# Hybrid layer with a top-4-of-32 expert FFN on one core: first norm without GpSimd, expert 0's rows in two banks, mixer matmuls reordered, another order of the tail

## The chip, the core and the metric

One core of a Trainium2 chip. The number is the device time of one execution, in microseconds (us). TensorE runs matmuls (its weight loads are counted apart), VectorE, ScalarE and GpSimd work on rows of 128 partitions, SyncE issues most DMAs. Kernels are compared by the median of several executions.

## The reference, cut to what matters

One layer in float32 on x of 512 tokens x 1024. Three mixers side by side share one input projection; their outputs are concatenated and projected, then a scaled residual and a LayerNorm; then 4 of 32 experts per token, and a second residual and LayerNorm.

```python
p = h @ w_in
mix = concat([pool_mixer(p), rwkv7_mixer(p), mlstm_mixer(p)]) @ w_out
h = layer_norm(ALPHA * h + mix, ln1_g, ln1_b)
logits = h @ router_w + router_b
top_val, top_idx = lax.top_k(logits, 4); gate = softmax(top_val)
# per expert e, over its tokens:
gu = xb @ w_gu[e] + b_gu[e]
act = glu * sigmoid(1.702 * glu) * (lin + 1)       # both halves clamped at 7
y[tokens] += gate * (act @ w_dn[e] + b_dn[e])
h = layer_norm(ALPHA * h + y, ln2_g, ln2_b)
```

## The kernel before, in words

Tokens are four tiles of 128 rows (NT = 4), features eight chunks of 128 (NK = 8). A scheduling layer orders each engine's instructions; engines then run their own list strictly in order, and wait on each other by semaphores. So the code says what depends on what, and the printed order of an engine says what stands behind a wait.

**Mixers** (up to about 347 us). The projection runs as three products of split halves (L222 to L224 for the transposed outputs, L249 to L251 for the others, in `ml_vo`). `rwkv_prep(j)` makes the operands of head pair j: two small products on a low-rank input (L559, L572), elementwise work on VectorE, a product that sums k*r for the "bonus" (L596), then `flip` transposes of v, b, k and a (L604, L613) and the state products (L618). `rwkv_scores(j)` makes per tile and head three or four 128x128 products over 64 partitions (L652); the two heads of a pair lie in partitions 0 to 63 and 64 to 127. A base loop of 31 VectorE steps (L693, L695) then inverts small blocks, a DMA and copies (L699 to L727) put its result in place, and matmuls go on with it (L756 and on). `ml_scores` does the like for the mLSTM heads.

**Output projection and first norm** (347 to 398 us). `out_proj(i, y, LATE)` adds the last part of the projection to the residual row tile `res[i]` on VectorE (L912). `ln_stats` takes mean and variance there (L1000, L1001) and an inverse root with ScalarE's Sqrt (L444 to L450); `ln_apply`, from `norm_rows`, scales on ScalarE (L1010), multiplies by the gain on VectorE (L1011) and adds the bias on GpSimd (L1012). The router works beside it (L1023 to L1056: logits, top 4, an expert mask `mkb` per tile at L1055). `route_rank` turns masks into the ranks of tokens, and those into the one-hot matrix `P0` (L1062 to L1067).

**Experts.** A ring of 18 buffers of 1 MiB holds the streamed weights: per expert eight chunks of w_gate_up and four of w_down, loaded by SyncE; a chunk's buffer is refilled when its matmuls are done. Expert e's tokens sit in 96 rows. For expert 0, `first_xT` gathers them by matmul of `res` with `P0` (L1231): tiles 0 and 1 into two banks, tile 2 into two more, tile 3 into two more, and VectorE adds the later ones (L1238). The others are gathered by indirect DMA. `gu` opens the accumulation with the bias through a one-hot `sel` (L1213, L1214, used at L1245, L1246); `gu_low` handles rows 0 to 63 (L1268), `gu_high` rows 64 to 95 (L1273), the latter after every fourth chunk. `dn` multiplies by w_down (L1309, L1314), and the scaled rows are scattered and added to `yd` in memory by GpSimd's DMA (L1319).

**Tail.** The last expert's rows never go to memory: `tail` multiplies them by one-hot matrices (L1524, L1527), per tile and half a group of two 128x512 and four 128x256 products in one bank. `tail_rows` has GpSimd's DMA queue add `yd` into `res` (L1507), with the loads of the second norm's gain and bias between. `overflow`, ahead of `tail`, holds code for experts with more than 96 tokens, behind a branch on the largest count (L1409); it does not run with these inputs, but each engine evaluates the branch. Then come residual sums (L1531), squares on ScalarE (L1537), scales, and an apply (L1557 to L1561) that is different for tiles 0, 1 and tiles 2, 3.

Of the kernel before, what the change touches and what calls it, by code (L numbers as in the profile page):

```python
# [126 lines left out]
class Trunk:  # L127
# [100 lines left out]
    def ml_vo(self):  # L228
# [9 lines left out]
        for q in (2, 0, 1):  # L238
# [4 lines left out]
            ps = [self.bank("pi" if i < 2 else "pm") for i in range(NT)]  # L243
# [114 lines left out]
    def ml_scores(self, i):  # L358
# [8 lines left out]
        for h in range(6):  # L367
            self.exp_ins = nc.scalar.activation(DW[:, h], DW[:, h], AF.Exp, bias=self.Q[:, i, 0, h:h + 1])
        for g in range(2):
            p = self.bank("pi")  # L370
            r = slice(64 * g, 64 * g + 64)
            for j in range(3):
                nc.tensor.matmul(p[:, j * 128:j * 128 + 128], self.k2[j][r, t], self.q2[j][r, t], start=True, stop=True)
            d = DW[:, g:6:2]
            nc.vector.scalar_tensor_tensor(d, p[:, :384].rearrange("p (j t) -> p j t", j=3), 1.0 / 32, d, OP.mult, OP.mult)
# [170 lines left out]
    def rwkv_prep(self, j):  # L546
# [12 lines left out]
        nc.tensor.matmul(p, self.w2t[0:64, j * 128:(j + 1) * 128], self.wdad[0:64], start=True, stop=True)  # L559
# [11 lines left out]
        pa = self.bank()  # L571
        nc.tensor.matmul(pa, self.w2t[64:128, j * 128:(j + 1) * 128], self.wdad[64:128], start=True, stop=True)  # L572
# [46 lines left out]
        for hh in range(2):  # L619
            rr = slice(64 * hh, 64 * hh + 64)  # L620
            for i in range(NT - 1):
                nc.vector.tensor_copy(self.H[i][rr, j], p[rr, 128 * i:128 * i + 128][:, rr])
        self.pj[j] = (at, bt, kt, cj)

    def rwkv_scores(self, j, first=False):
# [16 lines left out]
        for i in range(NT):  # L642
            ti = slice(i * 128, i * 128 + 128)
            tm = self.sp.tile([128, 2, 2, 128], F32, name="mkv", tag="mkv", bufs=2)
            (mab, mrb), yrk = self.M[i], self.Yrk[i]
            for hh in range(2):
                hd = 2 * j + hh
                rows = slice(64 * hh, 64 * hh + 64)
                p = self.bank()
                for q in range(1 if first else 0, 4):  # L650
                    lh, rh = prods[q]
                    nc.tensor.matmul(p[:, 128 * q:128 * q + 128], lh[rows, ti], rh[rows, ti], start=True, stop=True)  # L652
                pq = p.rearrange("p (q t) -> p q t", q=4)
# [236 lines left out]
    def out_proj(self, i, y, ks):  # L890
# [12 lines left out]
        r = self.res[i]  # L903
        for z in range(2):
# [4 lines left out]
            if ks is EARLY:  # L909
                nc.vector.scalar_tensor_tensor(r[:, c], r[:, c], ALPHA, p, OP.mult, OP.add)  # L910
            else:
                nc.vector.tensor_tensor(r[:, c], r[:, c], p, OP.add)  # L912
        if ks is LATE:
            self.mv[i] = self.ln_stats(self.sp, r)

    def norm_rows(self, i):
        self.ln_apply(self.res[i], self.mv[i], self.lng, self.lnb)
        self.nc.scalar.dma_start(self.hd[i * 128:i * 128 + 128], self.res[i])
# [210 lines left out]
    def routing_setup(self):  # L1129
# [5 lines left out]
        self.mkb = self.cp.tile([128, NT, NE], BF, name="mkb")  # L1135
        self.ro = self.cp.tile([128, 3, NT, 4], F32, name="ro")
# [53 lines left out]

    def expert_gather(self, e):
        x = self.xg[e % 2]
        self.nc.gpsimd.indirect_dma_start(out=x[0:CAP], out_offset=None, in_=self.hd,  # L1193
                                          in_offset=bass.IndirectOffsetOnAxis(ap=self.gidx[:, e:e + 1], axis=0),
                                          bounds_check=T - 1, oob_is_err=False)
# [15 lines left out]
    def expert_sel(self, e):  # L1211
        sel = self.mw.tile([128, 2, 128], F32R, name="sel", bufs=2)
# [5 lines left out]
    def first_xT(self):  # L1218
        nc = self.nc
        sel = self.expert_sel(0)  # L1220
        xT = self.mw.tile([128, NK, CAP], F32, name="xT", bufs=2)
        for tiles in ((0, 1), (2,), (3,)):
# [457 lines left out]
```

## Time and profile before

| | before |
|---|---|
| median of 3 runs | 1492.03 us (1488.74 to 1493.71) |
| profiled execution, its own time | 1492.41 us |
| its span (first to last instruction) | 1490.7 us |
| mean granted TensorE clock | 0.962 |
| TensorE busy | 1345.4 us, 90% of the span |
| VectorE, ScalarE, GpSimd busy | 466.6, 290.7, 228.2 us |
| moved by DMA | 461.67 MB |

How to read it: a busy share is a mean over stages with different limits, so the rows further down are taken by stage. "idle before" of a row is the time its engine stood still just ahead of it, with the instruction that ended it. The granted clock is a share of 2.4 GHz: 0.50 is 1.2 GHz. Matmul rows overlap: their durations do not add up to time, their distances do.

### The profile page before, as it was taken

The numbers are of one execution on the slowest core, as the hardware profiler recorded it, in microseconds if no ns is written. First come the engines' busy times: TensorE is split into PE (matmuls) and PEld (weight loads), VectorE is DVE, ScalarE is ACT, GpSimd is POOL, SyncE is SP. The second block draws the span as 40 slices with busy tenths as digits, with TensorE's granted clock in tenths as the row PEclk, the third lists the DMA queues.
The fourth block names the chain that finished last, engine by engine and source line by source line (L and its number), as shares of the span: only waits on it lengthen the run. The fifth ranks groups of instructions, "written<-read, shape, count | busy, mean of one in ns | idle before, by whom it ended". The sixth has DMA issues, their size and how long they took to land. (4 is left out here: it accounts for less than half of the span.)

```text
span 1490.7 us, 19988 instructions
## 1 busy us (share of the span) xinstructions
PE 1345.4 (90%) x7852; PEld 639.2 (43%) x7853; DVE 466.6 (31%) x1108; ACT 290.7 (20%) x611; POOL 228.2 (15%) x206
## 2 busy tenths in 40 slices
PE   7899989998899999988799999999879888899993
PEld 5677888876533433232233333333323222333322
DVE  4867497697831212111111111111111110211115
ACT  4444243353211111111001111111100110111103
POOL 1111137142301010001001111011100100010111
PEclk9999888799899999999999999999999999999996
DMA  7222123355689999999999999999999999999964
GB/s 250 70 57 71 36 68 89 118 159 205 256 341 396 393 383 404 402 398 390 395 399 398 394 398 399 402 395 391 392 387 398 395 401 394 404 396 412 401 223 127
DMA packets 95232, 461.67 MB, mean 310 GB/s; under 512 B 18137, under 2 KB 26745, under 8 KB 45962
## 3 DMA queue, kind: packets, MB, share of 16 engines
q1 hardware_dynamic: 79674, 434.57, 74.1%
q0 software_dynamic: 10880, 21.32, 6.6%
q10 hardware_dynamic: 4560, 4.15, 0.9%
q8 instruction: 82, 1.34, 0.4%
q14 instruction: 36, 0.29, 0.1%
HBM read 445.97 MB, written 18.10 MB: 311 GB/s over the span
## 5 line engine op out<-in xcount | busy, mean ns | idle before, releaser
L1268 PE MATMUL gu<-wc,xT 128*64 128x512 f32 x2048 | 486.6, 606 | 67.0 <-DMA wc<-w_gate_up 64.4
L1268 PEld LDWEIGHTS gu<-wc,xT 128*64 128x64 f32 x2048 | 143.0, 138 | 392.9 <-issue 239.5
L1281 DVE TENSOR_SCALAR glu<-gu 128x256 f32<-128x256 f32 (+1 forms) x64 | 35.6, 556 | 843.8 <-PE gu L1273 391.5
L1314 PE MATMUL dn<-wc,aT 128*64 128x512 f32 x1024 | 247.6, 603 | 4.2 <-PEq L1261 2.4
L1282 ACT ACTIVATE glu<-glu 128x256 f32<-128x256 f32 (+1 forms) x64 | 33.6, 525 | 549.6 <-DVE glu L1281 549.4
L1193 POOL DMA_INDIRECT xg<-hd,gidx x31 | 31.3, 1009 | 665.0 <-PE tr L1207 659.7
L1314 PEld LDWEIGHTS dn<-wc,aT 128*64 128x64 f32 x1024 | 65.8, 136 | 117.6 <-issue 101.3
L1319 POOL DMA_INDIRECT yd<-eo,sidx x45 | 70.1, 1557 | 276.1 <-ACT eo L1318 276.1
L1273 PE MATMUL gu<-wc,xT 128*32 128x512 f32 x960 | 111.3, 596 | 0.0
L222 PE MATMUL pi<-xhi,whi 128*128 128x512 f32 x152 | 63.7, 419 | 8.9 <-ACT whi L172 8.9
L1208 ACT ACTIVATE xT<-tr 128x384 f32<-128x384 f32 x62 | 29.9, 490 | 177.2 <-PE tr L1207 177.2
L223 PE MATMUL pi<-xlo,whi 128*128 128x512 f32 x152 | 62.8, 413 | 0.6 <-DVE xlo L173 0.6
L1273 PEld LDWEIGHTS gu<-wc,xT 128*32 128x32 f32 x960 | 27.7, 109 | 79.3 <-issue 79.3
L224 PE MATMUL pi<-xhi,wlo 128*128 128x512 f32 x152 | 61.7, 406 | 0.0
L173 POOL TENSOR_TENSOR wlo<-wraw,whi 128x512 fp32r<-128x512 f32 (+1 forms) x28 | 39.3, 1407 | 134.9 <-ACT whi L172 129.4
L1318 ACT ACTIVATE eo<-dn,gate 128x512 f32<-128x512 f32 (+1 forms) x45 | 28.0, 621 | 162.9 <-PE dn L1314 84.4
L1309 PE MATMUL dn<-wc,aT 128*32 128x256 f32 x960 | 56.1, 381 | 1.0 <-ACT aT L1296 1.0
L172 ACT ACTIVATE whi<-wraw 128x512 fp32r<-128x512 f32 (+1 forms) x54 | 33.9, 631 | 56.4 <-DMA wraw<-w_in 25.3
L1309 PEld LDWEIGHTS dn<-wc,aT 128*32 128x32 f32 x960 | 29.5, 110 | 33.3 <-issue 13.8
L1284 DVE SCALAR_TENSOR_TENSOR glu<-glu 128x256 f32<-128x256 f32 (+1 forms) x64 | 35.6, 556 | 8.4 <-ACT glu L1282 7.1
L1295 PEld LDWEIGHTS tr<-ident,glu 128*128 128x128 f32 x192 | 25.7, 208 | 28.0 <-DVE sel L1214 19.5
L222 PEld LDWEIGHTS pi<-xhi,whi 128*128 128x128 f32 x152 | 29.5, 194 | 18.2 <-ACT whi L172 8.6
(489 smaller groups left out, 1585.8 us busy)
## 6 DMA issues: line engine op xcount, KB each, us to landing
wc<-w_gate_up SPq DMA_DIRECT2D x256, 1024.0 KB
wc<-w_down SPq DMA_DIRECT2D x128, 1024.0 KB
wraw<-w_in SPq DMA_DIRECT2D x46, 256.0 KB
wraw<-w_out SPq DMA_DIRECT2D x16, 256.0 KB
xraw<-xT SPq DMA_DIRECT2D x4, 512.0 KB
res<-x SPq DMA_DIRECT2D x4, 512.0 KB
hd<-res ACTq DMA_DIRECT2D x4, 512.0 KB
res<-yd POOLq DMA_DIRECT2D x4, 512.0 KB
```

The source lines that it names most:

```text
L172: self.hi_ins = nc.scalar.activation(hi, src, AF.Copy)
L173: return (eng or nc.vector).tensor_tensor(lo, src, hi, OP.subtract)
L222: nc.tensor.matmul(p, hi, xh, start=(k == 0), stop=False)
L223: nc.tensor.matmul(p, hi, xl, start=False, stop=False)
L224: nc.tensor.matmul(p, lo, xh, start=False, stop=(k == NK - 1))
L1268: mm(p[q][64 * h:64 * h + 64], xT[:, k, 0:64], w[:, 1024 * q + 512 * h:1024 * q + 512 * h + 512], start=False, stop=(k == NK - 1))
L1273: self.nc.tensor.matmul(p[2][32 * c:32 * c + 32], xT[:, k, 64:96], w4[:, c], start=False, stop=(k == NK - 1), skip_group_check=True)
L1281: nc.vector.tensor_scalar(out[:, c], g, 7.0, None, OP.min)
L1284: nc.vector.scalar_tensor_tensor(out[:, c], ln[:, c], 1.0, out[:, c], OP.add, OP.mult)
L1309: mm(p2[32 * c:32 * c + 32], aT[:, 4 + k % 2, 32 * (k // 2):32 * (k // 2) + 32], wd[k][:, 256 * c:256 * c + 256], start=(k == 0), stop=(k ...
L1314: mm(p0[64 * h:64 * h + 64], aT[:, k % 4, 64 * (k // 4):64 * (k // 4) + 64], wd[k][:, 512 * h:512 * h + 512], start=(k == 0), stop=(k == N ...
L1319: return nc.gpsimd.indirect_dma_start(out=self.yd.rearrange("t (c f) -> (t c) f", f=w), out_offset=bass.IndirectOffsetOnAxis(ap=self.sidx[ ...
```

## The change

It does nine things. In `ml_vo` the first of three column groups takes its banks from another set. In `ml_scores` and `rwkv_scores` the products of two heads alternate, into two banks. In `rwkv_prep` both products on the low-rank input stand together, and the bonus product stands last. In the first norm, the residual add also sums the row, ScalarE makes squares of the centred row with a sum, and VectorE applies gain, scale and bias in two operations per half. `sel` of expert 0 is made during the setup of the router. `first_xT` sums all four tiles in two banks, and ScalarE copies them out. Expert 0's high rows are multiplied after each chunk. Gathers for e < 3 have no bounds check, and the fills of `xg` are gone. In the tail, the branch block moves behind it (and would redo residual and norm); the gain and bias are loaded by SyncE; for tiles 2 and 3 an identity matmul adds `res` in the bank, and ScalarE empties it with a sum; scale roots are taken for two tiles at once; all applying is VectorE's.

```diff
@@ ml_vo
-            ps = [self.bank("pi" if i < 2 else "pm") for i in range(NT)]
+            ps = [self.bank("ps" if q == 0 else "pi" if i < 2 else "pm") for i in range(NT)]
@@ rwkv_prep
         p = self.bank()
-        nc.tensor.matmul(p, self.w2t[0:64, ...], self.wdad[0:64], start=True, stop=True)
+        pa = self.bank()
+        for o, rows in ((p, slice(0, 64)), (pa, slice(64, 128))):
+            nc.tensor.matmul(o, self.w2t[rows, j * 128:(j + 1) * 128], self.wdad[rows], start=True, stop=True)
...
-        p = self.bank()
-        nc.tensor.matmul(p[32 * j:32 * j + 2], c["bd2"], r, start=True, stop=True)
-        nc.scalar.activation(self.bonT[32 * j:32 * j + 2], p[32 * j:32 * j + 2], AF.Copy)
...
+        p = self.bank()
+        nc.tensor.matmul(p[32 * j:32 * j + 2], c["bd2"], r, start=True, stop=True)
+        nc.scalar.activation(self.bonT[32 * j:32 * j + 2], p[32 * j:32 * j + 2], AF.Copy)
@@ rwkv_scores
+            ps = [self.bank() for _ in range(2)]
+            for q in range(1 if first else 0, 4):
+                lh, rh = prods[q]
+                for hh in range(2):
+                    rows = slice(64 * hh, 64 * hh + 64)
+                    nc.tensor.matmul(ps[hh][:, 128 * q:128 * q + 128], lh[rows, ti], rh[rows, ti], start=True, stop=True)
@@ out_proj, norm_rows
-                nc.vector.tensor_tensor(r[:, c], r[:, c], p, OP.add)
+                nc.vector.scalar_tensor_tensor(r[:, c], r[:, c], 1.0, p, OP.mult, OP.add, accum_out=self.mv[i][:, z:z + 1])
-            self.mv[i] = self.ln_stats(self.sp, r)
+            nc.vector.tensor_scalar(col(2), col(0), col(1), -1.0 / D, OP.add, OP.mult)
+            for z in range(2):
+                nc.scalar.activation(ps[z], r[:, 512 * z:512 * z + 512], AF.Square, bias=col(2), accum_out=col(6 + z))
+            nc.vector.tensor_scalar(col(5), col(6), col(7), 1.0 / D, OP.add, OP.mult)
+            self.rsqrt(col(3), col(5), 1e-5, col(4))
...
-        self.ln_apply(self.res[i], self.mv[i], self.lng, self.lnb)
+            self.nc.vector.scalar_tensor_tensor(r[:, c], r[:, c], mv[:, 2:3], self.lng[:, c], OP.add, OP.mult)
+            self.nc.vector.scalar_tensor_tensor(r[:, c], r[:, c], mv[:, 3:4], self.lnb[:, c], OP.mult, OP.add)
@@ first_xT
-        for tiles in ((0, 1), (2,), (3,)):
+        ps = [self.tbank() for _ in range(2)]
+        for i in range(NT):
...
+                nc.tensor.matmul(ps[k // 4][:, k % 4 * CAP:k % 4 * CAP + CAP], self.res[i][:, k * 128:k * 128 + 128], self.P0[:, i],
+                                 start=(i == 0 and k % 4 == 0), stop=(i == NT - 1), skip_group_check=True)
+        for q in range(2):
+            nc.scalar.activation(xT[:, 4 * q:4 * q + 4], ps[q][:, :4 * CAP].rearrange("p (k t) -> p k t", k=4), AF.Copy)
@@ experts
-        for x in self.xg:
-            self.nc.gpsimd.memset(x[0:CAP], 0.0)
-                if k % 4 == 3:
+                if e == 0:
+                    self.gu_high(p, k, t, w[k])
+                elif k % 4 == 3:
@@ tail, tail_rows, trunk
-            if i in (1, 2):
-                t, src = ((self.g2, self.a["ln2_g"]), (self.b2, self.a["ln2_b"]))[i - 1]
-                self.after(nc.gpsimd.dma_start(t, bass.AP(...)), d)
+                if i > 1:
+                    mm(p, self.ident, self.res[i][:, hs[q]], start=True, stop=False)
...
+                if i > 1:
+                    nc.scalar.activation(r[:, f], ps[i][q], AF.Identity, accum_out=col(q))
...
-                    nc.scalar.activation(r[:, f], r[:, f], AF.Identity, bias=col(8), scale=col(6))
-                    nc.vector.tensor_tensor(r[:, f], r[:, f], self.g2[:, f], OP.mult)
-                    nc.gpsimd.tensor_tensor(r[:, f], r[:, f], self.b2[:, f], OP.add)
+        for f, i in ((add, 0), (add, 1), (centre, 0), (add, 2), (centre, 1), (add, 3), (scales, 0), (apply, 0), (apply, 1),
+                     (centre, 2), (centre, 3), (scales, 2), (apply, 2), (apply, 3)):
+            f(i)
...
-                t.overflow()
                 t.tail(out)
+                t.overflow(out)
```

What this does to the order is seen on three lists. Line numbers of the changed kernel are higher (a flip is L602, L611 there, the bonus L622). First TensorE's list at head pair 0, where projections (pi), flips (ident) and the bonus product (out 2x512) share it; before:

```order
L222 MATMUL pi<-xhi_87,whi 128x512
L596 MATMUL ps<-M_232,cst 2x512
L604 MATMUL ps<-ident,M_233 128x128 x4
L604 MATMUL ps<-ident,prep 128x128 x8
L613 MATMUL ps<-ident,prep 128x128 x4
L494 MATMUL pm<-pbd 128x512
L618 MATMUL ps<-Vt,prep 128x128 x3
L223 MATMUL pi<-xlo_89,whi 128x512
```

and of the change:

```order
L602 MATMUL ps<-ident,M_233 128x128 x4
L222 MATMUL pi<-xhi_87,whi 128x512
...
L602 MATMUL ps<-ident,prep 128x128 x4
L222 MATMUL pi<-xhi_86,whi 128x512
...
L223 MATMUL pi<-xlo_88,whi 128x512
L602 MATMUL ps<-ident,prep 128x128 x4
L611 MATMUL ps<-ident,prep 128x128 x4
L224 MATMUL pi<-xhi_86,wlo 128x512
L616 MATMUL ps<-Vt,prep 128x128 x3
L622 MATMUL ps<-M_232,cst 2x512
```

The flips stood in one block right behind the bonus product; now the first stands 20 projection rows ahead of the last two, the second 8, and the bonus product is the last of the group.

Second, VectorE's list just ahead of expert 0, from the last expert mask (mkb) on; ohv rows are ranks and gates, cst rows become `P0`. Before:

```order
L1055 CAST mkb<-mkv 128x32
L1213 TENSOR_SCALAR sel<-cst 128x128
L1214 TENSOR_SCALAR sel<-cst 128x128
L1213 TENSOR_SCALAR sel<-cst 128x128
L1214 TENSOR_SCALAR sel<-cst 128x128
L1065 SCALAR_TENSOR_TENSOR ohv<-tr,mkb 128x1
L1067 COPY cst<-tr 128x32
L1066 TENSOR_SCALAR cst<-cst,ohv 128x96
L1094 TENSOR_REDUCE ohv<-ro 128x4
L1065 SCALAR_TENSOR_TENSOR ohv<-tr,mkb 128x1
L1067 COPY cst<-tr 128x32
L1066 TENSOR_SCALAR cst<-cst,ohv 128x96
```

and of the change:

```order
L1072 CAST mkb<-mkv 128x32
L1111 TENSOR_REDUCE ohv<-ro 128x4
L1232 TENSOR_SCALAR sel<-cst 128x128
L1112 RECIPROCAL ohv<-ohv 128x4
L1233 TENSOR_SCALAR sel<-cst 128x128
L1113 TENSOR_TENSOR ro<-ro,ohv 128x16
L1133 TENSOR_REDUCE ohv<-ohv 128x32 x2
L1134 COPY ohv<-ohv 128x64
L1082 SCALAR_TENSOR_TENSOR ohv<-tr,mkb 128x1
L1084 COPY cst<-tr 128x32
L1083 TENSOR_SCALAR cst<-cst,ohv 128x96
```

The rows of `sel` for expert 0 are gone (those that remain are expert 1's), and two reductions of L1133 with a copy stand ahead of the last rank (L1082 to L1083).

Third, TensorE's list in the tail; the branch is COMPARE_AND_BRANCH. Before, the rows around it, without the block that is jumped over:

```order
L1524 MATMUL dn_10532<-wc 128x512 x2
L1527 MATMUL dn_10532<-wc 128x256 x4
L1408 TENSOR_LOAD mxi
L1409 COMPARE_AND_BRANCH
...
L1409 UNCONDITIONAL_BRANCH x2
L1524 MATMUL gu_10489<-wc 128x512 x2
L1527 MATMUL gu_10489<-wc 128x256 x4
L1524 MATMUL gu_10490<-wc 128x512 x2
L1527 MATMUL gu_10490<-wc 128x256 x4
```

and of the change, from the second half of tile 2 on:

```order
L1539 MATMUL tr<-res_2757,ident 128x512
L1541 MATMUL tr<-wc 128x512 x2
L1544 MATMUL tr<-wc 128x256 x4
L1539 MATMUL dn_10001<-res_2757,ident 128x512
L1541 MATMUL dn_10001<-wc 128x512 x2
L1544 MATMUL dn_10001<-wc 128x256 x4
L1539 MATMUL dn_10002<-res_2757,ident 128x512
L1541 MATMUL dn_10002<-wc 128x512 x2
L1544 MATMUL dn_10002<-wc 128x256 x4
L1395 TENSOR_LOAD mxi
L1422 COMPARE_AND_BRANCH
```

Seven of eight groups stood behind the branch; now all eight stand ahead of it, and the groups of tiles 2 and 3 begin with an identity product (L1539).

## Rows read from the trace of the kernel before

**Rows 1.** Busy time by stretch, core 0; columns in the first line.

```profile
core 0: us, PE busy (x) PEld busy (x) DVE busy (x) ACT busy (x) POOL busy (x), PEclk, DMA share, GB/s
347.00:398.00 51.00, 38.27 (x258) 30.24 (x258) 43.80 (x126) 15.73 (x30) 16.67 (x13) 0.90 0.69 263
420.00:1430.00 1010.00, 938.84 (x5346) 323.34 (x5345) 136.19 (x311) 115.20 (x232) 98.32 (x74) 0.99 1.02 397
1454.00:1491.00 37.00, 10.95 (x52) 9.26 (x48) 21.21 (x56) 11.77 (x27) 6.38 (x4) 0.65 0.45 124
1459.00:1468.00 9.00, 5.36 (x19) 4.81 (x20) 1.61 (x5) 0.59 (x1) 0.00 (x0) 0.50 0.62 152
```

**Rows 2.** What TensorE waits for, 440 to 1460 us.

```profile
engine line waited for: us in total, times, longest us
PE gu L1268 <- DMA wc<-w_gate_up: 64.4, 75, 2.9
```

**Rows 3.** The same view, 0 to 165 us.

```profile
PE ps L596 <- DVE M L594: 7.4, 3, 3.7
```

**Rows 4.** Timeline of TensorE: start us, us, engine, line, operation, count.

```profile
161.22 0.38 PE L652 MATMUL ps<-Bt,prep 64*128 64x128 f32 x2
...
161.67 0.38 PE L652 MATMUL ps<-Bt,prep 64*128 64x128 f32 x2
...
169.96 0.48 PE L652 MATMUL ps<-R,prep 64*128 64x128 f32 x2
170.29 0.38 PE L652 MATMUL ps<-prep 64*128 64x128 f32 x2
```

**Rows 5.** TensorE's waits, 165 to 250 us, then timeline of VectorE and TensorE.

```profile
PE pi L249 <- ACT V L256: 6.7, 1, 6.7
...
187.82 0.69 DVE L291 SCALAR_TENSOR_TENSOR ks<-cv 128x512 f32<-128x512 f32 x1 [3.39 <-ACT cv L290]
...
241.32 1.43 DVE L727 COPY X<-bb 32x384 f32<-32x384 f32 x3
...
242.82 1.37 PE L756 MATMUL ps<-bb,M 32*32 32x32 f32 x47
```

**Rows 6.** Groups, 355 to 400 us: busy us, mean ns of one, idle before.

```profile
L1012 POOL TENSOR_TENSOR res<-res,ln 128x512 f32<-128x512 f32 x8 | 10.9, 1378 | 25.3 <-DVE lmv L447 12.8 <-DVE lmv L1003 6.4 <-DVE res L1011 4.0
...
L1052 DVE CAST ro<-i 128x4 f32<-128x4 uint32 x4 | 3.4, 857 | 0.0
...
L1056 DVE TENSOR_TENSOR ro<-mkv 128x4 f32<-128x4 f32 x4 | 2.3, 576 | 0.0
L448 DVE SCALAR_TENSOR_TENSOR lmv<-lmv 128x1 f32<-128x1 f32 x4 | 2.2, 552 | 0.0
...
L449 DVE SCALAR_TENSOR_TENSOR lmv<-lmv 128x1 f32<-128x1 f32 x4 | 0.6, 148 | 0.0
```

**Rows 7.** Timeline around expert 0's start.

```profile
389.88 0.18 DVE L1055 CAST mkb<-mkv 128x32 bf16<-128x32 f32 x1
...
390.25 0.79 PE L1245 MATMUL gu<-mb,sel 128*128 128x512 f32 x1 [4.02 <-DVE sel L1213]
...
398.39 3.65 PE L1268 MATMUL gu<-wc,xT 128*64 128x512 f32 x14
```

**Rows 8.** The tail: timeline, and the instructions of line L1409.

```profile
1462.64 1.19 PE L1524 MATMUL gu<-wc 128*128 128x512 f32 x2 [6.14 <-PEq L1409]
...
1470.16 0.63 PE L1524 MATMUL tr<-wc 128*128 128x512 f32 x2
...
1471.10 0.63 PE L1524 MATMUL dn<-wc 128*128 128x512 f32 x2
...
L1409 DVEq COMPARE_BRANCH  x1: 72/72/72, 1455.6 to 1455.6; - x1
L1409 PEldq COMPARE_BRANCH  x1: 6362/6362/6362, 1456.0 to 1456.0; - x1
...
1467.41 0.72 ACT L1537 ACTIVATE wc<-res,tst 128x512 f32<-128x512 f32 x1 [11.17 <-DVE tst L1535]
...
1477.91 2.29 DVE L1546 SCALAR_TENSOR_TENSOR wc<-res,tst,wc 128x512 f32<-128x512 f32 x2
...
1485.91 1.41 DVE L1557 SCALAR_TENSOR_TENSOR res<-wc,tst 128x512 f32<-128x512 f32 x2
```

More of the change, by code (lines that the diff above doesn't have):

```diff
@@ L368, in ml_scores @@
             self.exp_ins = nc.scalar.activation(DW[:, h], DW[:, h], AF.Exp, bias=self.Q[:, i, 0, h:h + 1])
+        ps = [self.bank("pi") for _ in range(2)]
+        for j in range(3):
+            for g in range(2):
+                r = slice(64 * g, 64 * g + 64)
+                nc.tensor.matmul(ps[g][:, j * 128:j * 128 + 128], self.k2[j][r, t], self.q2[j][r, t], start=True, stop=True)
         for g in range(2):
[L370 to L373, printed above, removed]
             d = DW[:, g:6:2]
-            nc.vector.scalar_tensor_tensor(d, p[:, :384].rearrange("p (j t) -> p j t", j=3), 1.0 / 32, d, OP.mult, OP.mult)
+            nc.vector.scalar_tensor_tensor(d, ps[g][:, :384].rearrange("p (j t) -> p j t", j=3), 1.0 / 32, d, OP.mult, OP.mult)
         if i < NT - 1:
@@ L645, in rwkv_scores @@
             (mab, mrb), yrk = self.M[i], self.Yrk[i]
+            ps = [self.bank() for _ in range(2)]
[4 more added lines that the diff above has]
+                    nc.tensor.matmul(ps[hh][:, 128 * q:128 * q + 128], lh[rows, ti], rh[rows, ti], start=True, stop=True)
             for hh in range(2):
                 hd = 2 * j + hh
[L648 to L653, printed above, removed]
+                pq = ps[hh].rearrange("p (q t) -> p q t", q=4)
                 if not first:
@@ L903, in out_proj @@
         r = self.res[i]
+        ps = []
+        if ks is LATE:
+            self.mv[i] = self.sp.tile([128, 8], F32, name="lmv", bufs=4)
         for z in range(2):
@@ L1389, in experts, with overflow @@
         self.dn(*pend)
-    def overflow(self):
+    def overflow(self, out):
         nc, tc = self.nc, self.tc
@@ L1407, in overflow @@
         self.nw = 0
-        most = nc.values_load(self.mxi[0:1, 0:1], min_val=0, max_val=T)
-        with tc.If(most > CAP):
+        with tc.If(self.most > CAP):
             nc.vector.memset(self.oone, 1.0)
@@ L1417, in overflow @@
             for i in range(NT):
+                r = self.res[i]
                 nc.sync.dma_start(self.ow[i][:, 0:1024], self.yo[i * 128:i * 128 + 128])
-                nc.vector.tensor_tensor(self.res[i], self.res[i], self.ow[i][:, 0:1024], OP.add)
-            nc.scalar.activation(self.warm, self.ow[3][:, 0:1], AF.Sqrt, bias=self.eps[1e-5], scale=0.0)
+                nc.vector.tensor_tensor(r, r, self.ow[i][:, 0:1024], OP.add)
+                self.ln_apply(r, self.ln_stats(self.mw, r), self.g2, self.b2)
+                d = nc.sync.dma_start(out[i * 128:i * 128 + 128], r)
+                for st in self.stores[i]:
+                    self.after(d, st, mybir.DependencyClass.Sync)
     def overflow_table(self):
@@ L1496, in tail_setup @@
         self.slast = [s[0][:, 1536:2048], self.chunk(F32R)[0][:, 0:512], s[1][:, 1536:1792], s[1][:, 1792:2048]]
+        s = self.chunk()[0]
+        self.g2, self.b2 = s[:, 0:1024], s[:, 1024:2048]
+        for t, src in ((self.g2, self.a["ln2_g"]), (self.b2, self.a["ln2_b"])):
+            nc.sync.dma_start(t, bass.AP(tensor=src.tensor, offset=src.offset, ap=[[0, 128], [1, D]]))
         for q, p in enumerate(self.P):
@@ L1527, in tail @@
                         mm(p[:, 256 * x:256 * x + 256], self.P[2 + 2 * q + x][:, t], self.slast[2 + z], start=False, stop=x == z == 1)
+        s = [self.chunk()[0] for _ in range(2)]
+        xs = [s[i // 2][:, 1024 * (i % 2):1024 * (i % 2) + 1024] for i in range(NT)]
+        self.stores = [[] for _ in range(NT)]
         def add(i):
```

85 lines of the change are left out of this document (29 added, 56 removed).

## Prediction

> **What bounds the kernel now.** I read the stretches first, then what TensorE waits for, then the places of the edits. From 420 to 1430 us TensorE is busy 938.84 of 1010 us and the DMA engines are full, at 397 GB/s [rows 1]: both the weight stream and the matmuls that take it are near their limit, and TensorE waits for w_gate_up 64.4 us in 75 pieces [rows 2]. None of the edits removes a byte or a matmul there. The ring of weight chunks is full before expert 0, and a chunk is replaced only when its matmuls are done, so **the whole stretch moves with the start of expert 0, one for one**, and an edit pays in two places only: what brings that start (398.39 us [rows 7]) forward, and what shortens the tail behind the last expert, 1454 to 1490.7 us, where TensorE is busy 10.95 of 37 us [rows 1]. Ahead of expert 0, the stretch from 347 to 398 us is VectorE's (43.80 of 51 us), TensorE's 38.27 [rows 1].
>
> The sum is made against the profiled execution, 1492.41 us, of which the span is 1490.7; the median of the runs, 1492.03, is 0.38 us lower, which I leave out. About 0.3% (4.5 us) is what a measurement of this kernel can tell from no change.
>
> **The mixers, part by part.** *Bonus product and flips.* TensorE waits 7.4 us in three pieces at L596 for VectorE's last product of each head pair [rows 3], with the flips and the state products behind it. Now the flips stand ahead, between projection matmuls, and the bonus comes last. It still stands at nearly the same projection matmul, but some 15 transposes now run ahead of it, so most of the wait is filled: of 7.4 us I take 5, ends 0 (the wait comes back at a flip) and 7.4. The second small product of rwkv_prep moves up beside the first on the same input: nothing, it waited for nothing before.
>
> *Pairs by row group.* The 88 score products are 176 matmul rows, of 64 partitions each. They start 0.16 us apart where one head runs alone (169.96 to 170.29, two in 0.33), and 0.11 where two heads happen to alternate (161.22 to 161.67, four in 0.45) [rows 4]. Alternating them all saves at most 176 x 0.05 = 8.8 us; at least nothing, since a pair now waits for two free banks. Many alternate already, and half the stretch waits for VectorE anyway: I take 2. *By the Trainium skill, TensorE: Matmul & The Clock Gate, section "Part 3: Packing small matmuls", products in different row groups run at the same time, whole, and not merely closer; by it the term would be the 8.8 us and the total 6.8 us lower. The trace shows overlap, but a spacing of 0.11 us and not a start together.* The same edit in ml_scores lies in a stretch where VectorE is the limit: nothing.
>
> *V and gate banks.* At L249 TensorE waits 6.7 us for ScalarE to empty a bank [rows 5]; with other banks it does not. But the next step, the inversion products (L756), starts at 242.82 us beside VectorE's copies L727 (241.32 to 243), which come from the base loop, not from L249 [rows 5]. So I take 2 of 6.7 us, ends 0 and 6.7. Cover of the rest: the base loop. If the projections ahead of it end earlier it starts earlier, since VectorE waits 3.39 us for the convolution of a projection just before it (187.82) [rows 5]; so the 5 and 2 us above do pass through it. Mixers together: **9 us**, ends 0 and 22.9.
>
> **First norm.** Per tile VectorE loses two row sums of squares and one aggregate, and gets two more 128x512 operations for scale and bias: equal within 0.2 us, and the tile's squares go to ScalarE, which loses two operations for it. GpSimd's eight L1012 leave (10.9 us, 1.38 each) [rows 6]. Beside them VectorE's tiny instructions stretch: L1052, L1056 and L448 take 857, 576 and 552 ns in the mean, L449 of the same size 148 [rows 6]. Excess: 4 x (857 + 576 + 552 - 3 x 148) = 6.2 us, all on the engine that is the limit there. New is a round trip: the second half of the norm waits for ScalarE's squares, two of 0.72 us each as in the tail [rows 8] with 0.2 us for reading the sum, 1.8 us. The order puts other tiles' rows between, so the last tile alone may show it. I take **6 us**, ends 0 (four round trips of 1.8 use it up) and 8 (a few more stretched kinds).
>
> **Expert 0's rows.** The last expert mask is ready at 390.06 (L1055), and the first matmul on weights starts at 398.39: 8.3 us [rows 7]. TensorE's 4.02 us wait for sel [rows 7] goes, but that only moves bias products into idle time. Removed from the path are the four sums L1238 and half of the products behind the last mask; against it, VectorE now has GpSimd-fed reductions ahead of the last tile's rank, an estimate of 1.5 us from the order of its rows. I take **2 us**, ends 0.6 and 3.4. Expert 0's high products by chunk free ring slots one at a time: TensorE's count is the same, the stream gains **1 us**, ends 0 and 4. The bounds check and the fills of xg cost nothing visible: off the path.
>
> **Tail.** Of the 36.5 us behind 1454.2: TensorE's products wait 6.14 us [rows 8], the jump over the overflow block (6362 ns on TensorE's queue, 72 on VectorE's) [rows 8]; now they stand ahead of it. Near the end two of VectorE's operations stretch to 2.29 us beside GpSimd's adds, where two otherwise take 1.41 [rows 8]; those adds go. New working: tiles 0 and 1, four groups of 0.94 us (1470.16 to 1471.10 [rows 8]) from 1455.3: 1459.1. By then rows 2 and 3 should have landed, since the two parameter loads no longer sit between them in GpSimd's queue. Tiles 2 and 3: four groups and four identity products, taken at 0.79 us, the row of a 128x512 product at L1245 [rows 7]: 3.8 + 3.2, 1466. ScalarE empties and squares tile 3, four operations with sums, 3.6: 1469.7. Scale chain some 1.2, four 128x512 operations for the last two tiles 2.8: 1473.7. From the last operation (1487.3) to the end it took 3.4 us [rows 8]: 1477.1, a gain of 13.6. Against that, TensorE's granted clock is 0.50, the lower level of 1.2 GHz, from 1459 to 1468 us, around its wait [rows 1]; products that wait for rows 2 and 3 may meet it too, so I take **11 us**, ends 5 (jump and landing both show at the end) and 14.
>
> **Sum:** 9 + 6 + 2 + 1 + 11 = 29: 1492.4 - 29 = **1463.4 us**.
>
> **Rivals.** *A. The mixers' gain stops at VectorE.* The base loop and the copies behind it stay where they are: 1492.4 - 20 = 1472.4. For it: rows 5's copies. Chance 0.22. *B. Tail alone.* ScalarE's round trips eat the norm's gain too, or the stream was the limit and gives nothing for an earlier start: 1481.4. Against it: the DMA engines are at a share of 0.69 up to 398 us, not 1.02 [rows 1], so there is room for an earlier start. Chance 0.13. *C. Slower: flips as in-order waits.* The 12 flips now stand among projection matmuls, in TensorE's one queue; each that comes before VectorE's operand stops the projections behind it, where one wait per head pair stood before. At the longest wait of rows 3, 3.7 us, twelve make 44 us, less the 7.4 that go and the other 24 of the sum: 1505. It decides from a mean wait of (24 + 7.4) / 12 = 2.6 us, which the 2.5 us mean of rows 3 nearly is. Against it: three of the four flips of a pair use operands that are made earlier than the bonus product. Chance 0.07. *D. The change does not do what it says:* order and waits come out as before, the jump only moves: within 0.3%. Chance 0.05. *E. The jump costs at the end.* VectorE and SyncE jump last of all; at the 6.4 us that TensorE's took, less the 3.4 us of the last store beside it, 3 us: 1466.4. Inside the forecast's case, 0.1 of its chance. *The Trainium skill, Runtime: NRT & Kernel Launch, section "Instruction fetch mechanics", has a taken branch to code outside the fetched window wait for a load of it: that agrees with TensorE's 6362 ns, and not with VectorE's 72.* *F. Pairs in full*, 6.8 us less: 1456.6, 0.08 of the forecast's chance.
>
> **How the numbers follow.** Forecast, with E and F: 0.50 (1452 to 1470); A 0.22; B 0.13; C 0.07; D 0.05; 0.03 for most upper ends at once (below 1446). The range of 8 in 10 runs from 1446 to 1483. Faster 0.50 + 0.22 + 0.13 + 0.03 = 0.88, same 0.05, slower 0.07.
>
> **What would show it.** Expert 0's first matmul at about 381 us (mixers and norm), 8.3 us from the last mask shrinking to 6; no 6 us wait in TensorE's tail; L1012's line gone and the small VectorE rows back at 0.15 us; the last operation some 19 us behind the last expert's end, not 33. Wrong would be: waits of TensorE at the flips, a new VectorE wait for ScalarE's squares, an unchanged start of expert 0, or a long jump behind the last store.

## The result, and the profile after

The changed kernel took 1466.94 us (median of four, 1463.89 to 1473.31) beside 1491.47 us of the kernel before: a ratio of 0.9842, 95% interval 0.9804 to 0.988. The profiled execution took 1463.89 us, its span 1462.1, and it is the shortest of the four; TensorE was busy 1332.6 us, VectorE 451.3, ScalarE 289.9, GpSimd 205.4; the mean granted clock was 0.978. The forecast was 1463.4, so the time is 3.5 us above it and inside the likeliest case. A second series of the same kernel (below) gave 0.9885, so the size is less sure than the sign.

Where the 28.6 us between the two spans came from, by the same events in both traces (us; "last w_down product" is the last one of the last expert):

| event | before | after | earlier by | gained in the stage |
|---|---|---|---|---|
| VectorE's base loop starts | 188.4 | 176.4 | 12.0 | 12.0 |
| first residual add of the first norm | 352.8 | 343.8 | 9.0 | -3.0 |
| last expert mask | 389.9 | 376.9 | 13.0 | 4.0 |
| first product on w_gate_up | 398.4 | 381.9 | 16.5 | 3.5 |
| last w_down product starts | 1453.8 | 1434.3 | 19.5 | 3.0 |
| end of the span | 1490.7 | 1462.1 | 28.6 | 9.1 |

Busy time by stretch of the changed kernel, columns as in rows 1:

```profile
330.00:381.00 51.00, 44.46 (x290) 34.42 (x289) 39.18 (x140) 15.83 (x37) 5.07 (x4) 0.97 0.77 289
...
400.00:1400.00 1000.00, 931.60 (x5310) 321.46 (x5308) 137.80 (x315) 115.32 (x233) 98.06 (x74) 1.00 1.02 395
...
1425.00:1463.00 38.00, 21.05 (x144) 11.49 (x142) 16.89 (x42) 11.77 (x30) 3.62 (x4) 0.87 0.51 122
```

Ahead of expert 0 GpSimd has almost gone (5.07 us) and VectorE is no longer the fullest engine; the stream is what it was, full DMA engines at 395 GB/s. What TensorE waits for, from 0 to 165 us:

```profile
PE ps L602 <- DVE prep L592: 2.2, 2, 1.1
PE ps L602 <- DVE prep L589: 2.1, 3, 0.7
PE ps L602 <- DVE M L504: 1.1, 1, 1.1
```

The same view, 165 to 250 us:

```profile
PE pi L222 <- ACT so L259: 7.0, 1, 7.0
PE pi L373 <- DVE ks L291: 5.0, 1, 5.0
```

The same view, 440 to 1462 us:

```profile
PE gu L1281 <- DMA wc<-w_gate_up: 61.0, 72, 2.9
PE tr L1539 <- DMA res<-yd: 2.5, 1, 2.5
```

The bonus product waits no more [rows 3], but the flips (L602) wait 5.4 us in six pieces. The wait of L249 for ScalarE [rows 5] has become one of L222 for ScalarE. The wait for VectorE's convolution (L373) was there before the change:

```profile
PE pi L373 <- DVE ks L291: 1.5, 1, 1.5
```

It differs between profiles of the same mixer code, from 1.5 to 5.0 us in those of before. In the tail one wait is new: for the rows that GpSimd's queue adds into `res`. Groups of the changed kernel from 340 to 382 us, columns as in rows 6:

```profile
L933 DVE SCALAR_TENSOR_TENSOR res<-res,lmv,ln 128x512 f32<-128x512 f32 x8 | 5.9, 743 | 0.0
...
L1069 DVE CAST ro<-i 128x4 f32<-128x4 uint32 x4 | 0.6, 161 | 0.0
L448 DVE RECIPROCAL lmv<-lmv 128x1 f32<-128x1 f32 x4 | 0.6, 158 | 0.4 <-ACT lmv L445 0.4
L449 DVE SCALAR_TENSOR_TENSOR lmv<-lmv 128x1 f32<-128x1 f32 x4 | 0.6, 152 | 0.0
L1073 DVE TENSOR_TENSOR ro<-mkv 128x4 f32<-128x4 f32 x4 | 0.6, 140 | 0.0
```

The cast that took 857 ns takes 161, the product that took 576 takes 140 [rows 6]; VectorE waits for ScalarE's round trip 0.4 us in all. Timeline around expert 0's start:

```profile
376.93 0.18 DVE L1072 CAST mkb<-mkv 128x32 bf16<-128x32 f32 x1
...
378.77 0.65 DVE L1133 TENSOR_REDUCE ohv<-ohv 128x32 f32<-128x128 f32 x2 [1.16 <-POOL ohv L1114]
...
381.91 1.94 PE L1281 MATMUL gu<-wc,xT 128*64 128x512 f32 x8
```

From the last mask to the first product it takes 5.0 us where it took 8.5, and VectorE waits 1.16 us for GpSimd in between. Timeline of the tail, then the branch over the overflow block (line L1422):

```profile
1434.60 1.20 PE L1541 MATMUL gu<-wc 128*128 128x512 f32 x4
...
1441.14 1.13 PE L1539 MATMUL tr<-res,ident 128*128 128x512 f32 x2 [2.53 <-DMA res<-yd]
...
1443.05 1.02 PE L1539 MATMUL tr<-res,ident 128*128 128x512 f32 x2
...
1445.76 0.21 DVE L1557 TENSOR_SCALAR tst<-tst 128x1 f32<-128x1 f32 x1 [2.83 <-ACT res L1554]
...
1453.53 2.74 DVE L1573 SCALAR_TENSOR_TENSOR wc<-wc,tst 128x512 f32<-128x512 f32 x4
...
L1422 SPq EVENT_SEMAPHORE  x9: 17/17/17, 1459.8 to 1460.4; - x9
...
L1422 PEldq COMPARE_BRANCH  x1: 3388/3388/3388, 1445.0 to 1445.0; - x1
...
L1422 DVEq COMPARE_BRANCH  x1: 76/76/76, 1454.2 to 1454.2; - x1
...
L1422 SPq COMPARE_BRANCH  x1: 45/45/45, 1456.7 to 1456.7; - x1
```

The products no longer wait for the branch [rows 8]. VectorE ends at 1456.3, 21.6 us behind the end of the last w_down product (1434.7), where some 19 were forecast and 33 stood before; the span ends 5.8 us later, where it took 3.4 before [rows 8].

### The profile page after: what moved, and what is told of

It is laid out like the page before. It is cut to its first block, busy times and chain, and to the rows that moved or that the text cites. A ratio compares the mean times of both kernels' runs of the same rounds, so it can differ in the third digit from the quotient of the medians.

```text
span 1462.1 us, 19978 instructions
## 1 busy us (share of the span) xinstructions
PE 1332.6 (91%) x7860; PEld 622.3 (43%) x7861; DVE 451.3 (31%) x1098; ACT 289.9 (20%) x621; POOL 205.4 (14%) x190
## 5 line engine op out<-in xcount | busy, mean ns | idle before, releaser
L1295 ACT ACTIVATE glu<-glu 128x256 f32<-128x256 f32 (+1 forms) x64 | 33.5, 524 | 542.0 <-DVE glu L1294 542.0
L222 PE MATMUL pi<-xhi,whi 128*128 128x512 f32 x152 | 65.3, 430 | 15.9 <-ACT whi L172 8.9
L222 PEld LDWEIGHTS pi<-xhi,whi 128*128 128x128 f32 x152 | 30.0, 198 | 26.3 <-ACT whi L172 8.6
L1308 PEld LDWEIGHTS tr<-ident,glu 128*128 128x128 f32 x192 | 25.5, 208 | 26.4 <-DVE sel L1233 19.5
```

The source lines that it names most:

```text
L222: nc.tensor.matmul(p, hi, xh, start=(k == 0), stop=False)
```

## The experiments

Eight kernels put one part of the change alone into the kernel before; four start from the changed one. "Base loop", "residual add" and "first product" are the events of the table. A single profile's events scatter by some us, so a stage is also given as a mean over kernels that share it.

**Score pairs alone.**

```diff
+            ps = [self.bank() for _ in range(2)]
...
+                for hh in range(2):
...
+                    nc.tensor.matmul(ps[hh][:, 128 * q:128 * q + 128], lh[rows, ti], rh[rows, ti], ...)
```

> The kernel before with the score products alternating by head (rwkv_scores and ml_scores) and nothing else. In the trace of the changed kernel the base loop starts 12.0 us earlier (176.4 against 188.43), 3.1 us of it ahead of the last head pair's scores and 8.9 within them, where the granted clock rose. Theory of the prediction: pairs are worth 2 us, so base loop and expert 0 start 2 us earlier and the time is 1489 to 1490. Rival, pairs carry the mixers: base loop 5 to 9 us earlier, expert 0 likewise, time 1482 to 1487. If neither, under 1 us, the 9 us within the scores need the other mixer edits.

1487.73 us, ratio 0.9987 (0.9969 to 1.0005). The base loop starts at 179.1, 9.3 us earlier, but the first residual add only 2.7 us. TensorE's timeline:

```profile
170.91 0.49 PE L652 MATMUL ps<-prep 64*128 64x128 f32 x4
171.24 0.39 PE L652 MATMUL ps<-R,prep 64*128 64x128 f32 x4
171.56 0.40 PE L249 MATMUL pi<-whi,xhi 128*128 128x268 f32 x1
```

Four products of two heads take 0.33 us, 0.08 each, where a single head's take 0.16 [rows 4]: two run in the time of one. That is what the Trainium skill, TensorE: Matmul & The Clock Gate, section "Part 3: Packing small matmuls", says, and not the 0.11 us that I took. But most of the 9.3 us is not this. The stretches of 5 us in the kernel before, columns as in rows 1:

```profile
165.00:170.00 5.00, 4.43 (x32) 3.67 (x30) 4.82 (x21) 4.21 (x10) 0.77 (x1) 1.00 0.26 82
170.00:175.00 5.00, 5.00 (x30) 4.47 (x31) 2.41 (x6) 0.45 (x2) 0.55 (x1) 0.67 0.66 123
175.00:180.00 5.00, 5.00 (x24) 4.28 (x20) 1.90 (x5) 0.45 (x2) 0.00 (x0) 0.50 0.08 10
```

and in the kernel with expert 0's rows alone, whose mixers are those of before:

```profile
165.00:170.00 5.00, 4.42 (x30) 3.66 (x29) 4.82 (x20) 4.21 (x10) 1.00 (x1) 1.00 0.26 82
170.00:175.00 5.00, 5.00 (x39) 4.22 (x39) 3.39 (x10) 0.89 (x4) 0.32 (x1) 1.00 0.66 124
175.00:180.00 5.00, 5.00 (x40) 4.62 (x40) 1.83 (x7) 0.45 (x2) 0.15 (x1) 1.00 0.07 9
```

In the kernel before the granted clock falls to 0.50 (1.2 GHz) while TensorE is busy all the time; in the other profile of the same mixer code it stays at 1.00, and the base loop starts at 181.7 rather than 188.4. So about 7 us of the shift is the clock, and 2.6 us (181.7 to 179.1) the pairs; both are differences of single profiles. None of the three cases on record came as a whole: the base loop moved as the rival had it, the time (1487.7) fell between the two.

**Bonus and flips alone**, with both products on the low-rank input side by side.

```diff
-        nc.tensor.matmul(p[32 * j:32 * j + 2], c["bd2"], r, start=True, stop=True)
...
+        nc.tensor.matmul(p[32 * j:32 * j + 2], c["bd2"], r, start=True, stop=True)
         self.pj[j] = (at, bt, kt, cj)
```

> The kernel before with the bonus product last and both low-rank products together (rwkv_prep), nothing else. Theory of the prediction: 5 us, base loop at about 183.4, expert 0 at about 393.4, time about 1487. Rival from the changed kernel's trace: TensorE's waits at the flips are there still (5.4 us at the flips where 7.4 stood at the bonus product), so 1 to 3 us only, time 1489 to 1491.

1484.37 us, ratio 0.9974 (0.9951 to 0.9997). The base loop starts at 179.0, the clock stays at 1.00 from 160 to 190 us, and the flips wait 2.2 + 2.0 + 1.9 = 6.1 us where the bonus product waited 7.4 [rows 3]:

```profile
PE ps L601 <- DVE prep L591: 2.2, 2, 1.1
PE ps L601 <- DVE prep L588: 2.0, 3, 0.7
PE ps L601 <- DVE M L503: 1.9, 2, 1.2
```

The gain against the 181.7 above is 2.7 us, not 5: the wait has mostly moved.

**V and gate banks alone.**

```diff
-            ps = [self.bank("pi" if i < 2 else "pm") for i in range(NT)]
+            ps = [self.bank("ps" if q == 0 else "pi" if i < 2 else "pm") for i in range(NT)]
```

> The kernel before with other banks for the first column group of ml_vo, nothing else. Theory of the prediction: 2 us, expert 0 at about 396.4. Rival: 0, because the copies behind the base loop end last; the inversion products then start within 0.5 us of 242.8. Second rival: the wait moves to another product on ScalarE, as the changed kernel shows 7.0 us of it at L222; then also 0.

1489.13 us, ratio 0.9996 (0.9971 to 1.002). TensorE's waits from 165 to 250 us:

```profile
PE pi L373 <- DVE ks L291: 3.9, 1, 3.9
PE pi L222 <- ACT so L259: 3.7, 1, 3.7
```

Of the 6.7 us of L249 [rows 5], 3.7 come back at the next projection, and L373 waits 3.9 instead of 1.5. That is the second rival: the wait moves. The time shows no gain, though its interval does not exclude the 2 us of the forecast.

**All mixer edits.** The three diffs above together.

> The kernel before with all mixer edits together. Theory of the prediction: 9 us, expert 0 at 389.4. From the changed kernel's trace, where the last residual add of the first norm came 10.7 us earlier: expert 0 at 387 to 389, time 1480 to 1483. If the edits add up, the three single runs' shifts sum to this one; if the shift here is larger than their sum by over 2 us, they work through one another (an order that fits, or a clock that stays up).

1482.79 us, ratio 0.9964 (0.9944 to 0.9985), 5.4 us. The first residual add stands at 344.3. Over the profiles it is at 352.4 in the mean of five kernels without mixer edits (348.7 to 357.0) and at 345.4 in six with all of them (343.3 to 348.4): 7.0 us. The ratios of the three single edits add up to 6.4 us, beside 5.4 here: no sign that they need each other.

**First norm alone**, with the fills of `xg` and the bounds check left off. The fills ran on GpSimd from 387.25 us on in the kernel before, just ahead of the last mask; their share was not taken apart.

```diff
-                nc.vector.tensor_tensor(r[:, c], r[:, c], p, OP.add)
+                nc.vector.scalar_tensor_tensor(r[:, c], r[:, c], 1.0, p, OP.mult, OP.add, accum_out=self.mv[i][:, z:z + 1])
...
+                nc.scalar.activation(ps[z], r[:, 512 * z:512 * z + 512], AF.Square, bias=col(2), accum_out=col(6 + z))
```

> The kernel before with the first norm on VectorE and ScalarE, no fills of xg and no bounds check for the first gathers. Theory of the prediction: small VectorE rows back at 0.15 us, expert 0 6 us earlier (392.4), time about 1486. From the changed kernel, where the last mask came 13.0 us earlier and the last residual add 10.7: 2 to 4 us, expert 0 at 394 to 396. Rival: ScalarE's squares make VectorE wait at L925, under 1 us.

1484.58 us, ratio 0.9962 (0.994 to 0.9983), 5.7 us. From the first residual add to the last mask it takes 33.5 us, before 37.1; from the mask to the first product 5.8, before 8.5. The 8.5 is a long one: in seven kernels without this edit and without that of expert 0's rows it takes 6.9 to 8.5, 7.8 in the mean, so this part is worth 2.0. It was not in my sum. TensorE's busy time by stretch, first the kernel before, around its last mask at 389.9:

```profile
383.00:390.00 7.00, 1.96 (x19) 1.70 (x18) 6.90 (x16) 2.37 (x4) 4.66 (x5) 0.77 0.80 272
390.00:398.40 8.40, 8.15 (x46) 7.36 (x46) 4.78 (x19) 0.00 (x0) 0.00 (x0) 0.58 0.70 292
```

and this kernel, around its last mask at 386.2:

```profile
383.00:386.00 3.00, 2.64 (x23) 2.55 (x22) 1.93 (x7) 1.06 (x3) 0.00 (x0) 0.81 0.97 348
386.00:392.00 6.00, 5.17 (x45) 4.56 (x42) 4.85 (x21) 0.00 (x0) 1.05 (x1) 1.00 0.96 367
```

Before, TensorE stood still for most of 7 us behind VectorE and then worked at 0.58; with a faster VectorE it has work up to the mask and the clock is 1.00. Between the mask and the first product the clock is 0.58 to 0.73 in the eight kernels without this edit, and 1.00 in all six with it.

**Expert 0's rows alone**, with `sel` of expert 0 made early.

```diff
-        for tiles in ((0, 1), (2,), (3,)):
...
+        ps = [self.tbank() for _ in range(2)]
+        for i in range(NT):
...
+        for q in range(2):
+            nc.scalar.activation(xT[:, 4 * q:4 * q + 4], ps[q][:, :4 * CAP].rearrange("p (k t) -> p k t", k=4), AF.Copy)
```

> The kernel before with expert 0's rows in two banks and its sel made early. Theory of the prediction: 2 us (0.6 to 3.4) from the last mask to the first product on weights, 8.3 us before, so 4.9 to 7.7. The changed kernel shows 5.0 us there. Rival: the wait on GpSimd's product in front of the last rank eats it, 0 us.

1489.15 us, ratio 0.9994 (0.9976 to 1.0012). From the mask to the first product it takes 8.1 us, inside the 6.9 to 8.5 of the kernels without this edit and the norm's: no gain that stands out of the scatter. Counted from the mask's end it is 7.9, outside the 4.9 to 7.7 expected. TensorE's timeline:

```profile
386.42 0.24 PE L1062 MATMUL tr<-mkb,onesb 128*128 128x32 bf16 x3 [3.77 <-DVE cst L1067]
...
387.10 6.53 PE L1230 MATMUL tr<-cst,res 128*128 128x96 f32 x32
```

The 4.02 us wait for `sel` [rows 7] is now one of 3.77 us for another row of VectorE, and the products behind it run at a granted clock of 0.55 (386.4 to 393.8 us): 32 take 6.53 us, where 16 take 1.92 in the changed kernel's trace.

**Expert 0's products by chunk alone.**

```diff
-                if k % 4 == 3:
+                if e == 0:
+                    self.gu_high(p, k, t, w[k])
+                elif k % 4 == 3:
```

> The kernel before with expert 0's high products after each chunk. Theory of the prediction: 1 us (0 to 4) by an earlier stream. The changed kernel's last product on w_gate_up came 19.5 us earlier and expert 0 only 16.5, so 3 us came in within the stream. If the chunks did that, expert 0 stays at 398.4 and the last product moves 2 to 4 us; if not, the 3 us are the stream's own spread between executions, and nothing moves.

1489.39 us, ratio 0.9995 (0.9975 to 1.0015). TensorE's waits for w_gate_up are 61.4 us in 67 pieces rather than 64.4 [rows 2]:

```profile
PE gu L1268 <- DMA wc<-w_gate_up: 61.4, 67, 2.9
```

Yet from the first to the last low product on w_gate_up (L1268) it takes 1031.1 us, within the 1030.7 to 1032.3 of the other kernels without this edit.

**The tail alone**, with the new order of `tail` and the loads of gain and bias moved; of its diff the last lines:

```diff
-                t.overflow()
                 t.tail(out)
+                t.overflow(out)
```

> The kernel before with the tail's edits alone. Theory of the prediction: 11 us (5 to 14), time about 1481. The changed kernel's tail, from the end of the last product of the experts to the end, took 27.4 us where 36.5 stood: 9.1 us, so 1482 to 1484. Nothing ahead of the tail should move by over 1 us.

1484.22 us, ratio 0.9952 (0.9929 to 0.9974), 7.2 us. From the start of the last w_down product to the end it takes 28.1 us; eight kernels with the old tail have 36.4 in the mean (35.9 to 36.8). Ahead of the tail nothing should have moved by over 1 us, but in this profile the first residual add comes 4.2 us later than before; the edit does not touch it.

**The changed kernel again**, without an edit, beside the next three.

> The changed kernel once more, as it is. In the profiles so far the granted clock between 160 and 190 us was 0.72 in five of six kernels whose score order is the one of before (the base loop then starts at 187 to 189 us), 1.00 in one (181.7), and 1.00 in four of four kernels with pairs, the bonus product last, or both. Theory: with the change the clock stays at 1.00 there (base loop at 176 to 177), so its executions spread less than those of before (1483 to 1495 us), and the ratio to before lies at 0.983 to 0.986. Rival: the clock's fall is chance in both, then a profile of the changed kernel can show it too, with the base loop at 183 or later.

1472.23 us (median of six, 1463.92 to 1476.53), ratio 0.9885 (0.9853 to 0.9917). The ratio expected, 0.983 to 0.986, was missed, and so was a smaller spread than that of the kernel before: it is 12.6 us. The base loop starts at 175.2, as in the first series' profile (176.4), and the clock from 160 to 190 us is 1.00, as expected; then the first residual add comes at 348.4 rather than 343.8. In between, from the first inversion product (L756 before, L758 here) to that add, TensorE runs the same number of products in every profile. First the first series' profile, then this one, columns as in rows 1:

```profile
230.19:343.84 113.65, 98.88 (x798) 85.98 (x798) 87.85 (x244) 44.63 (x114) 43.13 (x43) 0.85 0.44 143
228.48:348.43 119.95, 104.14 (x798) 90.22 (x798) 88.81 (x243) 44.85 (x115) 43.13 (x43) 0.80 0.42 140
```

Of the 6.3 us, 5.3 are TensorE's busy time at a lower granted clock, 1.0 its idle time. Over all 14 profiles this stretch takes from 109.2 us, at 0.88, to 120.0, at 0.80; the longer it is, the lower the clock (correlation -0.96).

**The overflow block ahead of the tail again**, as it was; of its diff the last lines:

```diff
+                t.overflow()
                 t.tail(out)
-                t.overflow(out)
```

> The changed kernel with the overflow block and its branch ahead of the tail, as before. Theory of the prediction: TensorE's wait at the jump is worth up to 6 us, so the time rises by 3 to 6 us against the changed kernel. Rival: TensorE waits for the rows of tile 2 anyway (2.5 us, until 1441.1) and the end of the program is 1.5 us shorter without the block's joins behind the last store, so 0 to 2 us more, or nothing.

1471.54 us, ratio 0.9882 (0.9853 to 0.9911). TensorE's timeline:

```profile
1443.48 0.77 PE L1537 MATMUL tr<-wc 128*128 128x512 f32 x1 [6.57 <-PEq L1422]
1444.05 1.05 PE L1537 MATMUL gu<-wc 128*128 128x512 f32 x2
```

The wait is back, and behind it the products run at a clock of 0.50 until 1449.2. From VectorE's last operation to the end it takes 3.3 us, not 5.8. From the start of the last w_down product to the end it takes 32.0 us, against 27.8 and 29.9 in the two profiles with the block behind: 2 to 4 us for the move. The times of the runs don't tell the two kernels apart; this profile gained 3.5 us by its first residual add (344.9, not 348.4), which the edit does not touch.

**Without the identity products.** VectorE adds all four tiles from the banks.

```diff
-                if i > 1:
-                    mm(p, self.ident, self.res[i][:, hs[q]], start=True, stop=False)
...
-                    nc.scalar.activation(r[:, f], ps[i][q], AF.Identity, accum_out=col(q))
```

> The changed kernel without the identity products: VectorE adds tiles 2 and 3 as it does tiles 0 and 1. In the changed kernel's tail each of the four identity products costs 0.85 us (a group takes 1.79 us, not 0.94), TensorE waits 2.5 us for rows with the products of tiles 2 and 3 behind the wait, and VectorE then stands 2.8 us for ScalarE. Theory: the identity products are a loss, the tail gets 2 to 4 us shorter. Rival: VectorE, with 16 operations of 0.69 us from there on, becomes the limit and gives it back: 0 to 1 us either way.

1468.46 us, ratio 0.9863 (0.9834 to 0.9892). Timeline of TensorE, then VectorE's last row:

```profile
1445.53 0.63 PE L1539 MATMUL tr<-wc 128*128 128x512 f32 x2
...
1446.47 0.63 PE L1539 MATMUL dn<-wc 128*128 128x512 f32 x2
...
1458.58 2.74 DVE L1568 SCALAR_TENSOR_TENSOR wc<-wc,tst 128x512 f32<-128x512 f32 x4
```

Groups follow each other by 0.94 us with no wait, where they take 1.79 with the identity product; the tail, counted as above, takes 26.7 us, against 27.8 and 29.9. In the profiles the products are a loss of 1 to 3 us; the intervals of the times overlap.

**Also the reduction behind the last rank.**

```diff
+        d = nc.vector.reduce_sum(G[:, 0:NE], self.V[:, i, :, 32:64].rearrange("p k e -> p e k"), axis=AX.X)
+        self.after(d, self.rank_ins)
```

> The kernel of the last run, and VectorE's reductions for the output start (L1133) held back until the last rank of expert 0 is made. In the changed kernel VectorE waits 1.16 us there for GpSimd's product, with the last rank behind it. Theory: expert 0 starts 1.2 to 1.9 us earlier (4.98 us from the last mask to the first product on weights become 3.1 to 3.8), and the time falls by as much against the last run. Rival: the two banks' earlier tiles (3.8 us of TensorE behind the masks) end last anyway, under 0.5 us.

1467.18 us (1461.52 to 1472.14), ratio 0.9863 (0.9834 to 0.9892): the lowest single time and the lowest median of its series, though its interval overlaps that of the changed kernel. TensorE's timeline around expert 0's start:

```profile
379.24 2.02 PE L1249 MATMUL tr<-cst,res 128*128 128x96 f32 x16
381.20 1.94 PE L1282 MATMUL gu<-wc,xT 128*64 128x512 f32 x8
```

VectorE's 1.16 us wait ahead of the rank is gone, but from the mask (376.4) to the first product it takes 4.8 us, 0.2 less, where 3.1 to 3.8 were expected. VectorE now waits 1.66 us there for TensorE's product of the rank (L1080), which stands behind the products of the tile before.

## Why the prediction was right, and where it was not

The bounds were read rightly. In the kernels without the edit by chunk the stretch on w_gate_up took 1030.7 to 1032.3 us, whether it began at 388 or at 403 us, so every gain ahead of expert 0 passed through one for one, as the forecast said. The sum of 29 us became 28.6 in the first pair of profiles. Over all profiles it is 7.0 (mixers) + 6.9 (norm and expert 0's rows) + 2.4 (chunks) + 7.8 (tail) = 24.1; the ratios of the five parts alone add up to 5.4 + 5.7 + 0.9 + 0.7 + 7.2 = 19.9, and the two series of the whole change give 24 and 17 us (1.58% of 1491.47, 1.15% of 1488.47). So the size was taken some 5 to 12 us too high, and some terms came near their size for reasons that they did not name; that part of the hit is luck.

**Mixers, 9 us: 7.0 measured, in large part for another reason.** "Most of the wait is filled" failed: the flips wait 5.4 of the 7.4 us. That is rival C's mechanism, with a mean of 0.9 us in six pieces, far from the 2.6 from which it decides. Two of 6.7 us for the banks failed: no gain is seen. The 2 us for pairs held in size (2.6), though its price per product did not: at 0.08 us rather than 0.11 the same sum gives up to 14 us (176 x 0.08), not the 8.8 of the upper end and of rival F, so most of that was not on the path. What no term held was the granted clock from 171 to 186 us, some 7 us; had I taken the stretch around 171 us apart, rows would have shown 0.50 there. In the means of the same profiles the base loop starts 10.9 us earlier and the inversion products 10.8; 3.8 us are lost between those and the residual add (115.4 us where it took 111.6), 2.5 of them idle time of TensorE. Rival A's mechanism did not hold, since the base loop moved; but its idea, that the gain is lost behind it, did for a third of it. Its price, 1472.4, is the median of the second series; that series does not show whether by this loss alone.

**First norm, 6 us, and expert 0's rows, 2 us: 6.9 measured of 8.** Together: from the first residual add to the first product 44.9 us in the mean of seven kernels without these edits, 38.1 in five with both. The stretched rows came back as said and ScalarE's round trip cost 0.4 us, but VectorE's part of the norm is 3.6 us; the other 2 us are TensorE's, which no longer stands still ahead of the last products and keeps its clock. That the norm's 6 us were met is so in part luck. Expert 0's rows gave 0.8 behind the norm (5.8 to 5.0), and alone nothing beyond scatter: near the lower end, 0.6. Forecast were 6 us from the mask's end to the first product, and 4.8 came.

**Chunks, 1 us.** Alone nothing; with all edits the stretch is 2.4 us shorter (1029.0 in the mean of five, 1028.0 to 1030.7). Why it gains only together is open.

**Tail, 11 us: 9.1 in the first pair, 7.8 in the mean of three profiles.** The products of tiles 0 and 1 and of 2 and 3 took what was said. Two steps failed. "By then rows 2 and 3 should have landed": by the trace's landing records the four tiles land 2.5 to 3.1 us apart, tile 2 at 1441.1 and tile 3 at 1443.6, and TensorE waited 2.5 us for tile 2. And the end, taken as 3.4 us, took 5.8. With these, 13.6 - 2.5 - 2.4 = 8.7. The clock, for which I deducted 2.6, stayed at 1.00 in this profile through the last products; in the second series it was 0.79 behind the same wait, and the tail 2 us longer. Rival E was right on the size (3 us, 2.4 measured), and the trace speaks for its way too. The branch's own row on SyncE is only 45 ns, but SyncE's next row begins 3.1 us behind it (1456.7 to 1459.8), and the semaphore that this row waits for was last updated at 1406.6: it is no wait that the profile shows. The same gap is 3.0 to 3.2 us in all five profiles with the block behind the tail. The last store lands in the same time (at 1459.3, 3.05 us behind VectorE's end, where it took 2.06 before), so how the 2.4 us divide between the two is open.

Left open: why the clock falls at 171 us in five of six kernels with the old order of scores and bonus and in none of eight with a new one; and what sets the clock between the inversion products and the first residual add, with which the profiles of the changed kernel differ most.

## What to carry to other kernels

A wait in an in-order queue is worth its length only if what stands behind it has nothing of its own to wait for: of 14 us of waits at the bonus product and the banks, 2 to 3 were gained. Look at the granted clock of short stretches before pricing an edit: where TensorE stands idle and then works at a low clock, as ahead of expert 0 (0.58), ending the idle time can also raise the clock behind it. Compare clocks over the same work, not over the same microseconds: from 230 to 250 us the granted clock is 0.61 in the changed kernel and 0.92 in the one before, yet over the first 20 us from the first inversion product on it is 0.61 and 0.60. In a tail, price the last landing of each input and each queue's jump at the end as terms of their own; a jump can cost more than its own row in the profile shows.

## What the runs showed of the hardware

- The granted clock fell to 0.50 with TensorE busy 5.00 of every 5 us, behind a wait of only 0.57 us at 169.37; with the same wait (0.58 us at 169.15) in another kernel of the same mixers it stayed at 1.00.
- Products on different halves of the partitions, in two banks, took 0.08 us each when they alternated, half of the 0.16 of one half alone.
- The row of the taken branch on TensorE's queue is 6167 to 6743 ns with the block ahead of the tail (nine profiles) and 3337 to 3926 with it behind (five); on the other queues it is 45 to 76. But on SyncE the next row stands 5.1 to 5.4 us behind the branch in the first case and 3.0 to 3.2 in the second, on a semaphore that was last updated before the branch. The Trainium skill, Runtime: NRT & Kernel Launch, section "Instruction fetch mechanics", has a branch out of the fetched window wait for a load; TensorE's and SyncE's rows agree, those of GpSimd (next row 0.4 us behind the branch) show no such wait.
- With the jumped-over block behind the tail, the end took 5.8 to 5.9 us after VectorE's last operation; with the block ahead, 3.3 to 3.4.
- Between the inversion products and the first residual add the same products took TensorE 98.9 us of busy time in one execution of the changed kernel and 104.1 in another, at a mean granted clock of 0.85 and 0.80.
